# An encoder trunk on one core: two weight splits moved behind a product, and the last tiles' scaling handed from VectorE to ScalarE

## The chip, the cores and the metric

The kernel runs on one core of one Trainium2 chip. The metric is device time in microseconds (us) of one execution; the figure for a kernel is the median of its runs. The engines of the core are named as the profile names them: PE (TensorE, matmuls), PEld (its weight loads), DVE (VectorE), ACT (ScalarE), POOL (GpSimd) and SP (SyncE, which issues most DMAs).

## The reference

Two sequences of 512 tokens with 1024 features each go through two layers in float32. Layer 0 mixes tokens by a two-dimensional Fourier transform, layer 1 by attention; each is followed by an MLP with a squared ReLU. At the end comes a norm.

```python
def sq_relu_mlp(h, w_up, w_down):
    a = jnp.maximum(h @ w_up, 0)
    return (a * a) @ w_down

def trunk(x, ...):
    for i in range(DEPTH):          # DEPTH = 2
        j = i // N_MIXERS
        if i % N_MIXERS == 0:
            x = x + fourier_mix(rms_norm(x, fourier_norm[j]), fourier_w_out[j])
        else:
            x = x + gqa_attention(rms_norm(x, attn_norm[j]), attn_w_qkv[j], ...)
        x = x + sq_relu_mlp(rms_norm(x, mlp_norm[i]), mlp_w_up[i], mlp_w_down[i])
    return rms_norm(x, final_norm)

def rms_norm(x, g):
    y = x * lax.rsqrt(jnp.mean(x * x, axis=-1, keepdims=True) + EPS)
    return y * g
```

## The kernel before, in words

**Split operands.** A float32 product is made of three matmuls on halves: each operand is written as a high part (ACT copies it to `float32r`) and a low part (DVE subtracts the high part from the original). `split` (L82, L83) does both. Raw weights come into the pool `rawp` (tag `raw`, five buffers) by a DMA on SP's queue (`load_raw`, L91). A buffer of it is free again when its last reader has run, so a load stands in SP's queue, in order, until some DVE or ACT instruction has finished. The split weights go into the pool `wp` (`own()`) or into slots of the activations' pool (`lent()`); these show as `w` and `u` in the profile.

**The end of layer 0's MLP.** `second_product` multiplies the squared activations by `w_down` in a scheme of seven products over two-by-two blocks. Its work is a list of items, one for each output block `m` from 0 to 3 in each group of inner blocks. An item's `Sums.go` runs five products of 12 matmuls each, in the order `t1`, `t3`, `t2`, `b22`, `t4`. The first and the fourth share one accumulator in PSUM, the second and the fifth another: the fourth can start only when DVE has added the first's result into the residual (L1135), and the fifth only when it has added the second's. PE's order is fixed by hand there; that of the other engines is chosen by a scheduler, which takes the instructions as their inputs come ready and by the place at which the code states them. During an item the raw weights of the next are loaded, summed (L1202 to L1204, L1210) and split.

Attention's first weights (the third third of `w_qkv`, keys and values, four tiles of 128x1024) are wanted when this MLP ends. The last group's items 2 and 3 each call `late()`, which loads two of them and splits them at once:

```python
    def late():
        for _ in range(2):
            wkv.append(load_w(w_qkv[2, len(wkv)], home=lent))
```

Behind them in SP's queue come a table for the rotary embedding (`rope`) and the weights of the first queries (`w_qkv[0, ...]`, split into `own()` buffers). When a block `m` is finished, DVE adds (L1299, L1300) and `ready` makes attention's operands (`make_h`, L86 on ACT and L87 on DVE) and the squares for its norm (L154 on ACT, L156 on POOL).

**The tail.** The last 256 tokens of the second sequence are made with the tokens on the partitions: `x` holds tokens 256 to 383 ("third tile", accumulators `o[0]`, `o[1]`), `z` tokens 384 to 511 (three accumulators `oz`, whose matmuls at L1761 are PE's last). All orders are by hand there. On DVE: the two adds that complete `x` (L1771), four `ob.write` (L1706, each followed by a DMA on SP), `add_group(0)` and `add_group(1)` (L1766), the steps of a reciprocal square root (L131 on ACT, L132 to L136 on DVE), and `scaled` (L1682), which multiplies by the norm's factor and the norm's weights `gf` in one instruction. ACT makes the sums of squares (L1676) and scales half a row of `z` (L1795). Three of the four last output halves leave from SP's queue, one from ACT's.

Of the kernel before, what the change touches and what calls it, by code (L numbers as in the profile page):

```python
# [11 lines left out]
F32 = mybir.dt.float32  # L12
F32R = mybir.dt.float32r
BF16 = mybir.dt.bfloat16
AF = mybir.ActivationFunctionType
# [3 lines left out]
P = 128  # L19
D = 1024  # L20
# [16 lines left out]
SUM_GROUPS = ((0, 4), (4, 4), (8, 4), (12, 4)), ((0, 2), (2, 4), (6, 4), (10, 4))  # L37
# [3 lines left out]
def trunk_kernel(ctx, tc, x_in, xt_in, y_out, dcos, dsin, feat, rope, gfour, gcol, grow, gfin,  # L41
                 w_four, w_nyq, w_qkv, w_o, w_up, w_row2, w_row4, w_sum2, w_sum4, w_down):
    nc = tc.nc
# [17 lines left out]
    def slot(shape, dt):  # L61
        return act.tile(shape, dt, tag="u4", name=nm("u"))
# [4 lines left out]
    def small(n=4):  # L67
        return sm.tile([P, n], F32, tag="s", name=nm("s"), padded_shape=[P, 8])
# [12 lines left out]
    def split(dst_hi, dst_lo, src, eng=nc.vector):  # L81
        nc.scalar.copy(dst_hi, src)  # L82
        eng.tensor_sub(dst_lo, src, f32(dst_hi))  # L83
# [5 lines left out]
    def load_raw(src, shape=(P, 1024)):  # L89
        raw = rawp.tile(list(shape), F32, tag="raw", name=nm("raw"))  # L90
        nc.sync.dma_start(raw, src)  # L91
        return raw
# [14 lines left out]
    def lent():  # L107
        return slot([P, 1024], F32R), slot([P, 1024], F32R)

    def load_w(src, eng=nc.vector, parts=1, home=own):  # L110
        raw = load_raw(src)
        w = home()
        for i in range(parts):
            sl = slice(i * 1024 // parts, (i + 1) * 1024 // parts)
            split(w[0][:, sl], w[1][:, sl], raw[:, sl], eng)
        return w
# [9 lines left out]
    def rsqrt_steps(out, ss, n, inv, more=None):  # L126

        v, s, y = [small(n)[:, :n] for _ in range(3)]
        stt = nc.vector.scalar_tensor_tensor
        return [  # L130
            lambda: nc.scalar.activation(s, ss, AF.Sqrt, scale=inv, bias=eps if more is None else more),  # L131
            lambda: nc.vector.tensor_scalar(v, ss, inv, EPS if more is None else more, ALU.mult, ALU.add),  # L132
            lambda: nc.vector.reciprocal(v, v),
            lambda: nc.vector.tensor_mul(y, s, v),
            lambda: stt(s, y, -0.5, s, ALU.mult, ALU.mult),
            lambda: stt(out, s, 1.5, y, ALU.add, ALU.mult),  # L136
        ]
# [529 lines left out]
    with tc.manual_schedule(engines={ET.PE, ET.Activation, ET.DVE, ET.Pool, ET.SP}):  # L667
# [127 lines left out]
        blocks = Blocks(0)  # L795
# [26 lines left out]
        rows = []  # L822
# [290 lines left out]
        for r in last:  # L1113
            r.go()

    def second_product(l, blocks, rows, late=lambda: None, ready=lambda m: None):
        e, new = [], [True] * 4
        there = set()

# [200 lines left out]
        if there_later:  # L1320
            rows, sums = items[0]
# [18 lines left out]
        else:  # L1340
            rows, sums = items[0]
# [17 lines left out]

        for k, (rows, sums) in enumerate(items):  # L1360
            nrows, nsums = items[k + 1] if k + 1 < len(items) else ([], None)
            if sums.g == len(SUM_GROUPS[l]) - 1 and sums.m > 1:
                late()
            with tc.manual_schedule(engines={ET.PE}):
                for r in rows:
                    r.first()
                    if r.m == 3:
                        change("b11", 0, r.g)
                for r in nrows:
                    r.load()  # L1370
                if k:
                    sums.split_3()
                hook()
                for i, op in enumerate(("t1", "t3", "t2", "b22", "t4")):
                    sums.go(i)
                    if sums.m == 3:
                        change(op, 1, sums.g)
                    if i == 0 and nsums:
                        nsums.load()
                    if i == 1:  # L1380
                        for r in rows:
                            r.second()
                            if r.m == 3:
                                change("b21", 0, r.g)
                        hook()
                        for r in nrows:
                            r.split()
                    hook()
                    if there_later and k == 0 and i in (2, 4):
                        change(ROW[i // 4], 0, 0)  # L1390
                    if i == 2 and nsums:
                        nsums.sum_123()
                        nsums.split_12()
                    if i == 3 and nsums:
                        nsums.sum_4()
                        nsums.split_4()
            for r in rows:
                finish(r.m)
            finish(sums.m)


    hT, rs, wkv = [[], []], [], []
# [3 lines left out]
        rsqrt(r, sums(q), NT, 1.0 / D)  # L1406
        rs.append(r)

    def late():
        for _ in range(2):  # L1410
            wkv.append(load_w(w_qkv[2, len(wkv)], home=lent))

    def operands(q, m):
        for fo in range(2 * m, 2 * m + 2):
# [181 lines left out]
    late = [qr[1, 2 + i % 2][:, 2 + i // 2] for i in range(4)]  # L1596
# [8 lines left out]
    for n in range(1, len(heads) + 1):  # L1605
        pts, nxt = [], []
        for t in range(NT):
# [3 lines left out]
            if n in (3, 5, 7, 9) and t == 0:  # L1611
                i = (n - 3) // 2
# [107 lines left out]
    with tc.manual_schedule(engines={ET.PE, ET.Activation, ET.DVE, ET.Pool, ET.SP}):  # L1720
        oa, ob, oc, oe = OutT(0, 4), OutT(1, 2), Out(), Out(3)
        for fo in range(KC):
            project(0, fo, ws, [a[0] for a in ats])
            square(0, fo)
            oa.gain(fo)
        xtok = [tokens(2, KC), tokens(3, 6)]
        for fo in range(KC):
            project(1, fo, ws, [a[1] for a in ats], 256)
            square(1, fo, 256)
            ob.gain(fo)  # L1730
            if fo == 1:
                oa.root()
            if fo == 3:
                oa.spread()
            if fo > 3:
                oa.write(fo - 4)
        x = xtok[0]
        o = ps(), ps()
        cols = slice(2 * P, 3 * P)
        for k in range(len(ats)):  # L1740
            ak, wk = ats[k][1], ws[k]
            for i in range(2):
                sl = slice(i * 512, (i + 1) * 512)
                mm3(o[i], ak[0][:, cols], ak[1][:, cols], wk[0][:, sl], wk[1][:, sl], k == 0, k == len(ats) - 1)
            if k == 1:
                ob.root()
        ob.spread()
        z = xtok[1]
        groups = ((0, 512), (512, 768), (768, 1024))
        oz = [ps() for _ in groups]  # L1750
        mm = nc.tensor.matmul
        for i, (c0, c1) in enumerate(groups):
            out = oz[i][:, : c1 - c0]
            if i == 2:
                for k in range(2):
                    mm(oz[2][:, k * P : (k + 1) * P], xt(1, 6 + k)[:, 3 * P :], ident, start=k == 0, stop=False,
                       skip_group_check=True)
            for k in range(len(ats)):
                (ah, al), (wh, wl) = ats[k][1], ws[k]
                for n, (lh, rh) in enumerate(((ah, wh), (ah, wl), (al, wh))):  # L1760
                    mm(out, lh[:, 3 * P :], rh[:, c0:c1], start=k + n + i // 2 == 0,  # L1761
                       stop=k == len(ats) - 1 and n == 2, skip_group_check=i == 2)

        def add_group(i):
            sl = slice(*groups[i])
            nc.vector.tensor_add(z[:, sl], oz[i][:, : groups[i][1] - groups[i][0]], z[:, sl])  # L1766
            oe.square(z[:, sl], i)

        h0, h1 = slice(0, 512), slice(512, 1024)
        for i, sl in enumerate((h0, h1)):  # L1770
            nc.vector.tensor_add(x[:, sl], o[i], x[:, sl])  # L1771
        oc.square(x)
        root = oc.root()
        ob.write(0)
        ob.write(1)
        add_group(0)
        for step in root[:3]:
            step()
        ob.write(2)
        for step in root[3:]:  # L1780
            step()
        ob.write(3)
        add_group(1)
        y, part = [slot([P, D], F32) for _ in range(2)], small(1)[:, 0:1]
        oc.scaled(y[0], x[:, h0], h0)
        nc.sync.dma_start(y_out[2][:P, h0], y[0][:, h0])
        nc.vector.tensor_mul(y[1][:, h0], z[:, h0], gf[:, h0])
        nc.vector.tensor_add(part, oe.ss[:, 0:1], oe.ss[:, 1:2])
        nc.vector.tensor_scalar(part, part, 1.0 / D, EPS, ALU.mult, ALU.add)
        oe.square(oz[2][:, :256], 2)  # L1790
        oc.scaled(y[0], x[:, h1], h1)
        nc.sync.dma_start(y_out[2][:P, h1], y[0][:, h1])
        for step in rsqrt_steps(oe.r, oe.ss[:, 2:3], 1, 1.0 / D, part):
            step()
        nc.scalar.activation(y[1][:, h0], y[1][:, h0], AF.Copy, scale=oe.r)  # L1795
        nc.scalar.dma_start(y_out[2][P:, h0], y[1][:, h0])
        oe.scaled(y[1], z[:, 512:768], slice(512, 768))
        oe.scaled(y[1], oz[2][:, :256], slice(768, 1024))
        nc.sync.dma_start(y_out[2][P:, h1], y[1][:, h1])
# [130 lines left out]
```

## Time and profile before

| | us |
|---|---|
| median of three runs | 1701.62 |
| the three runs | 1701.62, 1701.74, 1700.10 |
| the profiled execution | 1699.59 |
| its span, from first to last instruction | 1697.8 |
| PE busy | 1681.2 (99%) |
| DVE busy | 1234.2 (73%) |
| ACT busy | 854.9 (50%) |
| POOL busy | 333.4 (20%) |

The span is what the trace covers; the remaining 1.8 us of the execution lie around it. Times "at 706" are us from the start of the span. In rows of a timeline the columns are the start, the duration, engine, line, operation, output and inputs, shapes, and in brackets the idle time just ahead with the instruction that ended it.

### The profile page before, as it was taken

Reading aid. Unit: us, or ns where it says so; the run is one execution under the profiler, and the core shown is the slowest. Engines: PE = TensorE matmul, PEld = TensorE weight load, DVE = VectorE, ACT = ScalarE, POOL = GpSimd, SP = SyncE. Lnnn points to the kernel's source line nnn. Section 1 sums busy time; section 2 is a strip of 40 time slices with the busy share of each in tenths; the row PEclk is TensorE's granted clock in tenths of the full one; section 3 lists DMA queues with packets and bytes.
Section 4 is the critical chain, followed back from the end, with each engine's and each line's share of the span. In section 5 each row is a group of like instructions: output and inputs, shape, how many; then the busy total and the mean of one; then the engine's idle time right before and its main releaser. Section 6 shows DMA issues by size and latency. Waiting matters only on the chain. (4 is left out here: it accounts for less than half of the span.)

```text
span 1697.8 us, 21868 instructions
## 1 busy us (share of the span) xinstructions
PE 1681.2 (99%) x7845; PEld 1395.0 (82%) x7845; DVE 1234.2 (73%) x1809; ACT 854.9 (50%) x1487; POOL 333.4 (20%) x304
## 2 busy tenths in 40 slices
PE   9999999999999999999999999999999999999998
PEld 7987888888788888788888888788888888888887
DVE  8788776557887879876588744687755479787864
ACT  7566444456242424457787714654444544344234
POOL 1321443221000000232344303014422200000002
PEclk9999999999999999999999999999999999999999
DMA  9643555449454644611000213335544686555322
GB/s 337 169 149 113 197 189 182 151 169 390 173 201 146 216 143 175 227 53 34 18 25 1 100 60 127 104 120 195 183 143 154 224 310 229 164 207 189 124 75 100
DMA packets 103679, 265.81 MB, mean 157 GB/s; under 512 B 10177, under 2 KB 10177, under 8 KB 103570
## 3 DMA queue, kind: packets, MB, share of 16 engines
q1 hardware_dynamic: 87410, 232.69, 39.4%
q10 hardware_dynamic: 14256, 25.96, 4.0%
q0 software_dynamic: 1904, 5.77, 1.7%
q8 instruction: 61, 1.00, 0.2%
q14 instruction: 48, 0.39, 0.1%
HBM read 189.40 MB, written 73.92 MB: 155 GB/s over the span
## 5 line engine op out<-in xcount | busy, mean ns | idle before, releaser
L869 PE MATMUL ps<-u,w 128*128 128x512 f32 x4656 | 1065.8, 389 | 4.9 <-DVE w L83 2.5
L869 PEld LDWEIGHTS ps<-u,w 128*128 128x128 f32 x4656 | 872.4, 188 | 189.7 <-DVE w L83 4.1
L82 ACT CAST w<-raw 128x1024 fp32r<-128x1024 f32 (+1 forms) x224 | 217.4, 981 | 444.1 <-PE ps L869 261.4
L83 DVE TENSOR_TENSOR w<-raw,w 128x1024 fp32r<-128x1024 f32 (+1 forms) x224 | 255.1, 1142 | 59.5 <-ACT w L82 59.0
L156 POOL TENSOR_TENSOR t<-t,t 128x512 f32<-128x512 f32 (+1 forms) x56 | 77.6, 1385 | 737.2 <-ACT t L154 681.3
L83 DVE TENSOR_TENSOR u<-u,u 128x1024 fp32r<-128x1024 f32 (+1 forms) x131 | 156.2, 1219 | 21.3 <-ACT u L82 20.6
L82 ACT CAST u<-u 128x1024 fp32r<-128x1024 f32 (+1 forms) x131 | 131.5, 1044 | 72.4 <-PE ps L869 48.8
L77 PE MATMUL ps<-u,u 128*128 128x512 f32 (+2 forms) x388 | 150.2, 387 | 0.4 <-DVE u L83 0.4
L1135 DVE TENSOR_TENSOR u<-ps,u 128x512 f32<-128x512 f32 x160 | 109.5, 686 | 54.0 <-PE ps L869 53.2
L79 PE MATMUL ps<-u,u 128*128 128x512 f32 (+2 forms) x388 | 144.4, 372 | 0.0
L78 PE MATMUL ps<-u,u 128*128 128x512 f32 (+2 forms) x388 | 144.2, 372 | 0.0
L869 PE MATMUL ps<-u,u 128*128 128x512 f32 x576 | 137.6, 390 | 0.6 <-DVE t L960 0.5
L869 PEld LDWEIGHTS ps<-u,u 128*128 128x128 f32 x576 | 107.9, 188 | 24.1 <-issue 0.9
L986 POOL TENSOR_TENSOR u<-u 128x512 f32<-128x512 f32 x28 | 36.6, 1309 | 401.4 <-ACT u L885 401.4
L83 DVE TENSOR_TENSOR u<-ps,u 128x512 fp32r<-128x512 f32 (+4 forms) x118 | 74.7, 649 | 19.6 <-ACT u L82 18.5
L79 PEld LDWEIGHTS ps<-u,u 128*128 128x128 f32 x388 | 73.1, 188 | 13.0
L77 PEld LDWEIGHTS ps<-u,u 128*128 128x128 f32 x388 | 73.3, 189 | 10.7 <-DVE u L83 0.6
L78 PEld LDWEIGHTS ps<-u,u 128*128 128x128 f32 x388 | 73.4, 189 | 10.5
L82 ACT CAST u<-ps 128x512 fp32r<-128x512 f32 (+4 forms) x118 | 65.6, 561 | 27.1 <-PE ps L79 11.6
L947 DVE TENSOR_TENSOR t<-ps,u 128x512 f32<-128x512 f32 x30 | 20.7, 690 | 79.8 <-PE ps L869 58.0
L852 DVE TENSOR_TENSOR u<-ps,u 128x512 f32<-128x512 f32 (+1 forms) x48 | 30.9, 645 | 64.4 <-PE ps L79 64.4
L77 PE MATMUL ps<-u,w 128*128 128x512 f32 (+2 forms) x192 | 65.1, 339 | 0.0
(244 smaller groups left out, 1987.0 us busy)
## 6 DMA issues: line engine op xcount, KB each, us to landing
raw<-w_up SPq DMA_DIRECT2D x82, 512.0 KB, 4.5
u<-spill_t SPq DMA_DIRECT2D x60, 512.0 KB, 5.9
raw<-w_sum SPq DMA_DIRECT2D x56, 512.0 KB, 4.3
u<-spill_b SPq DMA_DIRECT2D x45, 512.0 KB, 5.2
spill_t<-u SPq DMA_DIRECT2D x87, 256.0 KB, 2.0
spill_b<-t ACTq DMA_DIRECT2D x60, 256.0 KB, 3.0
raw<-w_row SPq DMA_DIRECT2D x28, 512.0 KB, 4.1
park<-u SPq DMA_DIRECT2D x24, 512.0 KB, 3.2
```

The source lines that it names most:

```text
L77: nc.tensor.matmul(out, lh, rh, start=first, stop=False)
L78: nc.tensor.matmul(out, lh, rl, start=False, stop=False)
L79: nc.tensor.matmul(out, ll, rh, start=False, stop=last)
L82: nc.scalar.copy(dst_hi, src)
L83: eng.tensor_sub(dst_lo, src, f32(dst_hi))
L156: nc.gpsimd.tensor_add(acc[q][:, :n], acc[q][:, :n], s[:, :n])
L852: nc.vector.tensor_add(x[:, :n], o[:, :n], x[:, :n])
L869: nc.tensor.matmul(o, w[x][:, sl], h[k][y], start=first and k + i == 0, stop=k == n - 1 and i == 2, skip_group_check=not first)
L947: nc.vector.tensor_add(u2, ob, t[:, 0])
L986: eng.tensor_sub(t[:, 0], b12, b11)
L1135: nc.vector.tensor_add(x, o, x)
```

## The change

The first part cuts `late` in two. `late(False)` at the start of items 2 and 3 only loads two raw tiles; `late(True)` splits them, and is stated behind the fourth product of the same item, after the next item's `sum_4` and `split_4`. The second part reorders the tail. The third tile is multiplied by `gf` in one 128x1024 instruction ahead of `add_group(0)`; its two halves are then scaled by the norm's factor on ACT, in place of the two `scaled` on DVE. The second half's DMA goes to ACT's queue, `add_group(1)` moves into the steps of the first root, and `ob.write(3)` moves behind the sums for the second root, whose steps are cut in two around ACT's scaling.

```diff
-    def second_product(l, blocks, rows, late=lambda: None, ready=lambda m: None):
+    def second_product(l, blocks, rows, late=lambda split_them: None, ready=lambda m: None):
...
-            if sums.g == len(SUM_GROUPS[l]) - 1 and sums.m > 1:
-                late()
+            ending = sums.g == len(SUM_GROUPS[l]) - 1 and sums.m > 1
+            if ending:
+                late(False)
...
                     if i == 3 and nsums:
                         nsums.sum_4()
                         nsums.split_4()
+                    if i == 3 and ending:
+                        late(True)
...
-    def late():
+    wraw = []
+
+    def late(split_them):
         for _ in range(2):
-            wkv.append(load_w(w_qkv[2, len(wkv)], home=lent))
+            if split_them:
+                wkv.append(lent())
+                split(*wkv[-1], wraw[len(wkv) - 1])
+            else:
+                wraw.append(load_raw(w_qkv[2, len(wraw)]))
...
         oc.square(x)
+        y, part = [slot([P, D], F32) for _ in range(2)], small(1)[:, 0:1]
         root = oc.root()
         ob.write(0)
         ob.write(1)
+        nc.vector.tensor_mul(y[0], x, gf)
         add_group(0)
         for step in root[:3]:
             step()
         ob.write(2)
+        add_group(1)
         for step in root[3:]:
             step()
-        ob.write(3)
-        add_group(1)
-        y, part = [slot([P, D], F32) for _ in range(2)], small(1)[:, 0:1]
-        oc.scaled(y[0], x[:, h0], h0)
+        nc.scalar.activation(y[0][:, h0], y[0][:, h0], AF.Copy, scale=oc.r)
         nc.sync.dma_start(y_out[2][:P, h0], y[0][:, h0])
         nc.vector.tensor_mul(y[1][:, h0], z[:, h0], gf[:, h0])
         nc.vector.tensor_add(part, oe.ss[:, 0:1], oe.ss[:, 1:2])
         nc.vector.tensor_scalar(part, part, 1.0 / D, EPS, ALU.mult, ALU.add)
         oe.square(oz[2][:, :256], 2)
-        oc.scaled(y[0], x[:, h1], h1)
-        nc.sync.dma_start(y_out[2][:P, h1], y[0][:, h1])
-        for step in rsqrt_steps(oe.r, oe.ss[:, 2:3], 1, 1.0 / D, part):
+        ob.write(3)
+        root = rsqrt_steps(oe.r, oe.ss[:, 2:3], 1, 1.0 / D, part)
+        for step in root[:3]:
+            step()
+        nc.scalar.activation(y[0][:, h1], y[0][:, h1], AF.Copy, scale=oc.r)
+        nc.scalar.dma_start(y_out[2][:P, h1], y[0][:, h1])
+        for step in root[3:]:
             step()
         nc.scalar.activation(y[1][:, h0], y[1][:, h0], AF.Copy, scale=oe.r)
         nc.scalar.dma_start(y_out[2][P:, h0], y[1][:, h0])
```

What the scheduler made of the first part is seen in DVE's order. This is DVE in item 2, before; `raw_5751` and `raw_5757` are the first two tiles of `w_qkv`, the `w_` rows split the next item's weights, and L1135 are the adds that free PE's accumulators:

```order
L1204 TENSOR_TENSOR raw_5784<-raw_5784,raw_5782 128x512
L83 TENSOR_TENSOR u_5754<-raw_5751,u_5753 128x1024
L1135 TENSOR_TENSOR u_4004<-ps_5786,u_4004 128x512
L83 TENSOR_TENSOR u_5760<-raw_5757,u_5759 128x1024
L83 TENSOR_TENSOR w_5818<-raw_5814,w_5818 128x1024
L1135 TENSOR_TENSOR t_3730<-ps_5800,t_3730 128x512
L1210 TENSOR_TENSOR raw_5782<-raw_5782,raw_5814 128x512
```

and the same place on DVE in the changed kernel, where the two tiles are `raw_5751` and `raw_5753`:

```order
L1204 TENSOR_TENSOR raw_5776<-raw_5776,raw_5774 128x512
L83 TENSOR_TENSOR w_5810<-raw_5806,w_5810 128x1024
L1135 TENSOR_TENSOR u_4004<-ps_5778,u_4004 128x512
L1210 TENSOR_TENSOR raw_5774<-raw_5774,raw_5806 128x512
L83 TENSOR_TENSOR u_5831<-raw_5751,u_5830 128x1024
L1135 TENSOR_TENSOR t_3730<-ps_5792,t_3730 128x512
L83 TENSOR_TENSOR w_5827<-raw_5774,w_5827 128x512
L83 TENSOR_TENSOR u_5835<-raw_5753,u_5834 128x1024
```

The next item's weights and L1210 now stand ahead of the two splits, which move down by three and by four rows. A little further, where item 2 ends and item 3 begins, DVE has before (`raw_6493` is the first weight of the queries, `raw_5861` and `raw_5867` the third and fourth tile; `ps_5878` and `ps_5892` are the results of item 3's first and second product):

```order
L1299 TENSOR_TENSOR u_3668<-u_3668,t_3730 128x512
L83 TENSOR_TENSOR w_6495<-raw_6493,w_6495 128x1024
L87 SCALAR_TENSOR_TENSOR u_5857<-u_3668,gc,u_5857 128x512
L83 TENSOR_TENSOR u_5864<-raw_5861,u_5863 128x1024
L1135 TENSOR_TENSOR u_4118<-ps_5878,u_4118 128x512
L83 TENSOR_TENSOR u_5870<-raw_5867,u_5869 128x1024
L1135 TENSOR_TENSOR u_4118<-ps_5892,u_4118 128x512
```

and now (`ps_5870` and `ps_5884` are those two results):

```order
L1299 TENSOR_TENSOR u_3668<-u_3668,t_3730 128x512
L1135 TENSOR_TENSOR u_4118<-ps_5870,u_4118 128x512
L87 SCALAR_TENSOR_TENSOR u_5857<-u_3668,gc,u_5857 128x512
L83 TENSOR_TENSOR w_6495<-raw_6493,w_6495 128x1024
L83 TENSOR_TENSOR u_5926<-raw_5861,u_5925 128x1024
L1135 TENSOR_TENSOR u_4118<-ps_5884,u_4118 128x512
L83 TENSOR_TENSOR u_5930<-raw_5863,u_5929 128x1024
```

The add of the first product moved ahead of the queries' weight and of a split; the add of the second stands behind both as before. PE's and POOL's orders are unchanged, and SP's is changed in the tail alone. ACT's casts follow DVE's new order. One thing of SP's queue is not seen in its order: the third tile's buffer is now the one that L1210 frees, the fourth's the one that the first of the deferred splits frees, and the load of `raw_6493` waits for the second deferred split, where before it waited for the split of `raw_5782`.

In the tail, ACT had before (L1676 are sums of squares, `s_14149` is the third tile's factor, `s_14151` the last tile's):

```order
L1676 ACTIVATE t_14604,s_14150<-u_14312 128x256
L1676 ACTIVATE t_14614,s_14150<-ps_14540 128x256
L131 ACTIVATE s_14619<-s_14150,s_14608 128x1
L1795 ACTIVATE u_14607<-u_14607,s_14151 128x512
L1796 DMA y<-u_14607 128x512
```

and has now (L1685 is that L1676, L1808 that L1795):

```order
L1685 ACTIVATE t_14603,s_14150<-u_14312 128x256
L1794 ACTIVATE u_14583<-u_14583,s_14149 128x512
L1685 ACTIVATE t_14613,s_14150<-ps_14540 128x256
L131 ACTIVATE s_14618<-s_14150,s_14585 128x1
L1804 ACTIVATE u_14583<-u_14583,s_14149 128x512
L1805 DMA y<-u_14583 128x512
L1808 ACTIVATE u_14584<-u_14584,s_14151 128x512
L1809 DMA y<-u_14584 128x512
```

Two scalings and one DMA issue came to ACT, one of the scalings ahead of the third sum of squares and one ahead of the last scaling.

## The prediction

> **What bounds the kernel.** I read the page's parts 1 and 4 first, then PE's waits, then PE's and DVE's rows around the two places that the change touches.
>
> ```profile
> span 1697.8 us, 21868 instructions
> PE 1681.2 (99%) x7845; PEld 1395.0 (82%) x7845; DVE 1234.2 (73%) x1809; ACT 854.9 (50%) x1487; POOL 333.4 (20%) x304
> ```
>
> PE is idle for 1697.8 - 1681.2 = 16.6 us in all, so a saving must come out of these or of the end behind PE's last matmul. From 700 us on PE waits for others only three times:
>
> ```profile
> PE ps L869 <- DVE u L1135: 1.5, 1, 1.5
> PE ps L869 <- DVE u L224: 0.9, 1, 0.9
> PE ps L1524 <- POOL t L1518: 0.2, 1, 0.2
> ```
>
> The columns are the total, the number of times and the longest. The first lies in item 3 of the MLP's last group:
>
> ```profile
> 647.80 58.87 PE L869 MATMUL ps<-u,w 128*128 128x512 f32 x259
> 708.14 5.74 PE L869 MATMUL ps<-u,w 128*128 128x512 f32 x24 [1.47 <-DVE u L1135]
> 713.72 0.39 PE L77 MATMUL ps<-u,u 128*128 128x512 f32 x1
> ```
>
> One matmul starts (58.87 - 0.39) / 258 = 0.2267 us behind the other, so the next would have started at 647.80 + 259 x 0.2267 = 706.51. It is the first of the fourth product, which waits until DVE has added the first product's result. Twenty-four matmuls on, attention would have begun at 711.95, not at 713.72: the stall costs 1.77 us. Its cause is in DVE's queue:
>
> ```profile
> 690.75 1.21 DVE L83 TENSOR_TENSOR u<-raw,u 128x1024 fp32r<-128x1024 f32 x1
> 691.89 0.68 DVE L1135 TENSOR_TENSOR u<-ps,u 128x512 f32<-128x512 f32 x1
> 692.49 1.94 DVE L83 TENSOR_TENSOR u<-raw,u 128x1024 fp32r<-128x1024 f32 x1
> ...
> 697.59 0.69 DVE L83 TENSOR_TENSOR w<-raw,w 128x512 fp32r<-128x512 f32 x1 [0.16 <-ACT w L82]
> ...
> 699.93 1.22 DVE L1300 TENSOR_TENSOR u<-u,t 128x1024 f32<-128x1024 f32 x1
> 701.06 0.68 DVE L1135 TENSOR_TENSOR u<-ps,u 128x512 f32<-128x512 f32 x1
> 701.78 0.69 DVE L1299 TENSOR_TENSOR u<-u,t 128x512 f32<-128x512 f32 x1
> 704.46 1.23 DVE L83 TENSOR_TENSOR w<-raw,w 128x1024 fp32r<-128x1024 f32 x1 [1.99 <-ACT w L82]
> 705.61 0.74 DVE L87 SCALAR_TENSOR_TENSOR u<-u,gc,u 128x512 fp32r<-128x512 f32 x1
> 706.27 1.22 DVE L83 TENSOR_TENSOR u<-raw,u 128x1024 fp32r<-128x1024 f32 x1
> 707.40 0.68 DVE L1135 TENSOR_TENSOR u<-ps,u 128x512 f32<-128x512 f32 x1
> ```
>
> The add that PE wants is the row at 707.40. Its product was done at 706.51 - 24 x 0.2267 = 701.07 and a little, but ahead of it stands the first weight of the queries, for whose high part DVE idles 1.99 us, because ACT waits for the load:
>
> ```profile
> 703.38 1.05 ACT L82 CAST w<-raw 128x1024 fp32r<-128x1024 f32 x1 [4.88 <-DMA raw<-w_qkv]
> 698.30 2.06 SPq L91 DMA_DIRECT2D raw<-w_qkv  x2
> ```
>
> The second row is the issue: 703.38 - 698.30 = 5.08 us from issue to cast.
>
> The tail, from PE's last matmuls to the last DMA:
>
> ```profile
> 1684.54 1.27 DVE L1706 TENSOR_TENSOR u<-u,ps 128x512 f32<-128x512 f32 x2
> 1686.88 0.69 DVE L1766 TENSOR_TENSOR u<-ps,u 128x512 f32<-128x512 f32 x1 [1.07 <-PE ps L1761]
> 1688.61 0.16 DVE L134 TENSOR_TENSOR s<-s,s 128x1 f32<-128x1 f32 x1 [0.19 <-ACT s L131]
> 1689.67 0.42 DVE L1766 TENSOR_TENSOR u<-ps,u 128x256 f32<-128x256 f32 x1
> 1690.01 0.74 DVE L1682 SCALAR_TENSOR_TENSOR u<-u,s,gf 128x512 f32<-128x512 f32 x1
> 1690.66 0.68 DVE L1787 TENSOR_TENSOR u<-u,gf 128x512 f32<-128x512 f32 x1
> 1691.52 0.74 DVE L1682 SCALAR_TENSOR_TENSOR u<-u,s,gf 128x512 f32<-128x512 f32 x1
> 1692.18 0.20 DVE L132 TENSOR_SCALAR s<-s,s 128x1 f32<-128x1 f32 x1
> 1693.67 0.48 DVE L1682 SCALAR_TENSOR_TENSOR u<-ps,s,gf 128x256 f32<-128x256 f32 x1
> 1690.60 0.36 ACT L1676 ACTIVATE t<-ps 128x256 bf16<-128x256 f32 x1
> 1693.27 0.72 ACT L1795 ACTIVATE u<-u,s 128x512 f32<-128x512 f32 x1 [1.27 <-DVE s L136]
> 1694.02 0.39 ACTq L1796 DMA_DIRECT2D y<-u  x1
> 1694.18 0.33 SPq L1799 DMA_DIRECT2D y<-u  x1
> ```
>
> From 1686.88 to 1694.15 (1693.67 + 0.48) DVE idles once, 0.19 us: these 7.27 us are DVE's own instructions, one behind the other, and the last DMA leaves 0.03 us later. ACT has holes all along.
>
> **Part one, the splits.** Nothing is added or removed; two pairs of casts and subtractions move. The early loads are issued as before. DVE's new order from 690.75 on is: weight split, add, L1210, deferred split, add, half-size split, deferred split. With starts spaced as in the rows (1.14 for 1024 columns, 0.60 for 512) that is 3 x 1.14 + 4 x 0.60 = 5.82, to 696.57. Until here it is the old work without the 0.73 by which the split at 692.49 exceeded the one at 690.75. Next come L87 and an add (0.66 and 0.60), a weight split (1.14), L1300 (1.13), the add that waits (0.72 from 701.06 to 701.78) and L1299 (0.60): 4.85, to 701.42. There now stands the first product's add, whose result is there, and it ends at 702.1, 4.4 us before PE wants it at 706.51. The deferred splits cost nothing: their reader is attention's first product at 711.95, some 15 us later.
>
> What is late next is the second product's add. The fifth product wants it at 706.51 + 12 x 0.2267 = 709.23, and it still stands behind the queries' weight. That load now waits for the second deferred split, so it is issued at about 696.6, not 698.30. I keep 5.08 us to the cast: 701.7. Behind the cast (0.96 to the next row's start, as from 703.38 to 704.34) ACT scales an operand (0.72), which DVE's L87 needs: 703.4. L87, the weight split, a split and the add take 0.66 + 1.14 + 1.14 + 0.68: DVE is done at 707.0, 2.2 us early. The third tile's load, now behind L1210, goes out at about 693.2 in place of 692.0, and its reader in this chain comes at 705.2, 12 us on.
>
> So the whole 1.77 us should go. From below the bound is the new wait at the fifth product, which eats it from a landing at 703.9 on; from above, the 1.77 itself. I take 1.77. It reaches the end because PE waits for only 0.9 + 0.2 us more behind this place; the nearest margin that could eat it is the softmax loop's, where POOL's 0.2 us wait shows how close it runs, and its inputs come from PE, which shifts them too.
>
> These four loads come closer together (693.2 to 696.6 in place of 692.0 to 698.3). One more price is open, DVE against POOL:
>
> ```profile
> 689.04 1.79 DVE L1204 TENSOR_TENSOR raw<-raw,raw 128x512 f32<-128x512 f32 x1
> 692.05 1.29 POOL L156 TENSOR_TENSOR t<-t,t 128x512 f32<-128x512 f32 x1 [1.77 <-ACT t L154]
> 706.67 4.18 POOL L156 TENSOR_TENSOR t<-t,t 128x512 f32<-128x512 f32 x2 [13.32 <-ACT t L154]
> ```
>
> An instruction of 512 columns took 1.79 us in place of 0.68, and the split at 692.49 took 1.94 in place of 1.21, both beside a POOL addition. By these rows a collision costs DVE 0.73 to 1.11, and the two additions of the last row, which will come some 1.7 us earlier and so beside the weight split and the add, at most 2.2: the margin, just. The Trainium skill's page "SBUF — State Buffer", section "Who interferes with whom", says that a VectorE instruction with two SBUF inputs and a GpSimd one that reads SBUF exclude each other for a whole instruction. The trace agrees in kind. By that rule two collisions could cost 2 x 1.29 = 2.6, and PE would wait 0.4 us at the fifth product: a sum of 2.9 in place of 3.3.
>
> **Part two, the tail.** The product with `gf` costs one 128x1024 instruction (1.22 by the L1300 row, 1.14 to the next start). It starts at 1685.74, when the two L1706 are through, in DVE's wait of 1.07 us for PE, and lets the next start at 1686.88: exactly PE's release. Cost 0 to 0.1. Out of DVE's 7.27 us fall two L1682 (1690.01 to 1690.66 and 1691.52 to 1692.18: 0.65 + 0.66). The 0.19 wait for ACT's root goes as well, since the 256-column add (0.34) now stands ahead of it. The other rows only change places. Sum 1.50.
>
> ACT gets two scalings (0.72 each by L1795) and one more DMA issue (0.39). The first waits for the factor, which comes at about 1689.3 (three root steps behind the moved add), and ends by 1690.0; the third sum of squares follows and ends by 1690.4. DVE wants that at 1692.18 - 1.50 = 1690.68: 0.3 us to spare. The second scaling and its issue end at about 1691.7, when the last factor arrives. So ACT's last scaling ends at 1692.5, and its DMA leaves beside SP's at 1692.7; the transfers behind are the same, 1.5 us earlier. If ACT ran 0.72 later, the DVE end would lose 0.4, so the bounds are 1.0 and 1.6. I take 1.50.
>
> **The sum.** 1.77 + 1.50 = 3.27 us. The profiled execution took 1699.59 and would take 1696.3; the median of the runs stands 2.03 above it, so 1701.62 - 3.27 = 1698.35, or 1698.3. The measurement tells about 0.2% from no change, which is 3.4 us: the forecast lies right at that edge.
>
> **The rivals.**
> 1. The wait moves to the fifth product. For it: DVE still idles for the same load there, and POOL's additions fall in. Against it: 2.2 us of margin. With half the gain left, 0.9 + 1.5 = 2.4: 1699.2.
> 2. The 1.77 is lost further on, in the softmax loop or at L224. For it: POOL's wait at L1524. Against it: one wait of 0.2 us in a loop that PE feeds. Then only the tail counts: 1700.1.
> 3. ACT becomes the tail's bound through the added scaling and issue. Against it: the holes above. 1.77 + 1.0 = 2.8: 1698.8.
> 4. Slower: the queries' weight lands late, because four 512 KB loads now follow in 3.4 us. A landing beyond 703.9 (7.3 us after issue) costs PE one for one. The kernel gets slower than before only from 707.2 on, and by over 0.2% from 710.6, 14 us after issue. L91's loads took 11.7 us at most:
>
> ```profile
> DMA to landing us min/median/max: 2.5/4.3/11.7
> ```
>
> **How the numbers follow.** The main case has 0.65, rival 1 0.14, rival 2 0.09, rival 3 0.08, rival 4 0.04. In the main case 3.27 lies just below the edge of 3.4, and the three runs spread over 1.6 us, so I give 0.40 of its 0.65 to faster. A little of rival 3 goes there too: faster 0.42, same 0.54, slower 0.04. The main case alone is 1697.0 to 1699.2; for eight in ten I take in rivals 1 and 2 and the spread of runs: 1696.7 to 1700.4.
>
> **What would show it.** Right: PE's only long waits behind 700 us are those for L224 and L1524; L77 begins near 711.95; DVE's wait for the queries' weight stands behind the first add; the last SP issue comes 5.8 us behind the last L1761, where it was 7.3. Wrong: a wait for L1135 in the middle of item 3, an ACT row that ends DVE's idle time ahead of the second L132, or a new PE wait in attention.

## The result, and the profile after

| | us |
|---|---|
| before, median of 17 runs | 1700.06 (1699.27 to 1701.74) |
| after, median of 17 runs | 1697.31 (1696.56 to 1698.75) |
| ratio after to before | 0.9984, 95% interval 0.9978 to 0.9990 |
| the profiled execution of after, and its span | 1697.05, 1695.3 |

The change takes 2.75 us away; the interval makes that 1.7 to 3.7 us. The first three runs of before, with their median of 1701.62, had come out high: over 17 runs it stands at 1700.06.

The page of after, parts 0 and 1, and what PE waits for behind 700 us:

```profile
span 1695.3 us, 21868 instructions
PE 1681.1 (99%) x7845; PEld 1395.1 (82%) x7845; DVE 1231.3 (73%) x1808; ACT 854.8 (50%) x1489; POOL 334.6 (20%) x304
```

```profile
PE ps L869 <- DVE u L224: 0.9, 1, 0.9
PE ps L1533 <- POOL t L1527: 0.2, 1, 0.2
```

PE has the same work. The wait for L1135 is gone; the two others are those of before (line numbers behind `late` are 9 to 13 higher now). The end of the MLP in PE's timeline:

```profile
699.12 13.12 PE L869 MATMUL ps<-u,w 128*128 128x512 f32 x57
712.08 0.39 PE L77 MATMUL ps<-u,u 128*128 128x512 f32 x1
```

Fifty-seven matmuls at 0.2267 us end at 699.12 + 12.92 = 712.04; attention begins 0.04 later, 1.64 us ahead of the first trace. DVE there, then the load that it waits for, on SP and ACT:

```profile
692.54 1.18 DVE L1210 TENSOR_TENSOR raw<-raw,raw 128x512 f32<-128x512 f32 x1
...
695.98 1.22 DVE L83 TENSOR_TENSOR u<-raw,u 128x1024 fp32r<-128x1024 f32 x1
...
701.98 0.69 DVE L1135 TENSOR_TENSOR u<-ps,u 128x512 f32<-128x512 f32 x1
704.44 0.75 DVE L87 SCALAR_TENSOR_TENSOR u<-u,gc,u 128x512 fp32r<-128x512 f32 x1 [1.78 <-ACT u L86]
705.11 1.22 DVE L83 TENSOR_TENSOR w<-raw,w 128x1024 fp32r<-128x1024 f32 x1
706.25 2.32 DVE L83 TENSOR_TENSOR u<-raw,u 128x1024 fp32r<-128x1024 f32 x1
708.49 0.68 DVE L1135 TENSOR_TENSOR u<-ps,u 128x512 f32<-128x512 f32 x1
```

```profile
697.23 2.72 SPq L91 DMA_DIRECT2D raw<-w_qkv  x2
702.74 1.05 ACT L82 CAST w<-raw 128x1024 fp32r<-128x1024 f32 x1 [5.71 <-DMA raw<-w_qkv]
```

The first product's add (701.98) now stands ahead of the wait for the queries' weight and ends at 702.67; the fourth product is due at 699.12 + 33 x 0.2267 = 706.60, 3.9 us later. The second's (708.49) ends at 709.17. PE's fifth product is due at 699.12 + 45 x 0.2267 = 709.32, so 0.15 us of margin is left.

The tail, DVE, then ACT, SP and PE:

```profile
1684.51 1.22 DVE L1786 TENSOR_TENSOR u<-u,gf 128x1024 f32<-128x1024 f32 x1
1685.66 0.69 DVE L1775 TENSOR_TENSOR u<-ps,u 128x512 f32<-128x512 f32 x1
...
1688.77 0.68 DVE L1715 TENSOR_TENSOR u<-u,ps 128x512 f32<-128x512 f32 x1
1689.54 0.21 DVE L132 TENSOR_SCALAR s<-s,s 128x1 f32<-128x1 f32 x1
...
1691.04 0.48 DVE L1691 SCALAR_TENSOR_TENSOR u<-ps,s,gf 128x256 f32<-128x256 f32 x1
```

```profile
1689.03 0.38 ACT L1685 ACTIVATE t<-ps 128x256 bf16<-128x256 f32 x1 [0.28 <-PE ps L1770]
...
1691.64 0.35 ACTq L1809 DMA_DIRECT2D y<-u  x1
```

```profile
1691.55 0.33 SPq L1812 DMA_DIRECT2D y<-u  x1
```

```profile
1687.26 1.67 PE L1770 MATMUL ps<-w,u 128*128 128x256 f32 x12
```

From the first add to SP's last issue it takes 1691.55 - 1685.66 = 5.89 us, where it was 7.30: 1.41 less. ACT's last issue comes 0.09 us later and is now the end, so 1.32 us is gained. ACT's third sum of squares starts when PE's last matmul ends (1687.26 + 1.67 = 1688.93), and DVE waits 0.09 us for it ahead of the last root.

### The profile page after: what moved, and what is told of

It is laid out like the page before. It is cut to its first block, busy times and chain, and to the rows that moved or that the text cites. A ratio compares the mean times of both kernels' runs of the same rounds, so it can differ in the third digit from the quotient of the medians.

```text
span 1695.3 us, 21868 instructions
## 1 busy us (share of the span) xinstructions
PE 1681.1 (99%) x7845; PEld 1395.1 (82%) x7845; DVE 1231.3 (73%) x1808; ACT 854.8 (50%) x1489; POOL 334.6 (20%) x304
## 5 line engine op out<-in xcount | busy, mean ns | idle before, releaser
L156 POOL TENSOR_TENSOR t<-t,t 128x512 f32<-128x512 f32 (+1 forms) x56 | 77.8, 1389 | 738.9 <-ACT t L154 683.0
L1135 DVE TENSOR_TENSOR u<-ps,u 128x512 f32<-128x512 f32 x160 | 109.5, 686 | 53.5 <-PE ps L869 53.0
```

The lines of the kernel that those rows point to most:

```text
L156: nc.gpsimd.tensor_add(acc[q][:, :n], acc[q][:, :n], s[:, :n])
L1135: nc.vector.tensor_add(x, o, x)
```

## The experiments

**Each part by itself.** In `splits_only` the tail is the text of before; in `tail_only` the splits are.

> Part one alone: the two split pairs moved, the tail as before. Theory A (the stall's 1.7 us reaches the end, save what a later place eats): PE shows no wait for L1135 in item 3, attention begins 1.7 us earlier, and the kernel is 1.2 to 1.7 us faster than before. Rival B (the stall's time is lost before the tail): the first matmul of the tail is less than 0.5 us earlier and the time is within 0.5 us of before. Separately: in the trace with both parts PE lost 0.4 us again between 1389 and 1418 us (layer 1's MLP, where DVE waits for w_sum loads). If that comes from the new order, this trace loses 0.4 us there too; if it comes from how the loads happen to land, it need not.

> Part two alone: the splits as before. Theory A: the last DMA issue comes 2.6 us behind PE's last matmul, where it was 4.0 us; the kernel is 1.4 us faster (1.3 to 1.5), since nothing else moves. Rival C (ACT's added scaling and issue bound the end): 1.0 us or less, and DVE waits for ACT ahead of the last root. The stall of 1.77 us at the fourth product of item 3 is still there. Between 1389 and 1418 us nothing is lost if the loss of 0.4 us belongs to the new order of the splits.

| | median, us | before beside it | ratio, 95% interval |
|---|---|---|---|
| splits_only | 1698.86 (11 runs) | 1699.82 (33 runs) | 0.9991, 0.9982 to 1.0000 |
| tail_only | 1698.46 (11 runs) | 1699.82 (33 runs) | 0.9991, 0.9982 to 1.0000 |

0.96 and 1.36 us: together 2.3, near the 2.75 of both. Each interval reaches from 0 to 3.1 us, so these times alone tell neither part from no change, nor one part from the other; what each is worth rests on the traces. The tail gives what was expected. The last issue in `tail_only` is ACT's:

```profile
1692.94 0.36 ACTq L1800 DMA_DIRECT2D y<-u  x1
```

It comes 2.99 us behind the start of PE's last matmul (1689.95), where in the first trace it was 1694.18 - 1689.88 = 4.30, so 1.31 less. The splits give less than expected. PE's timelines, `tail_only` (old order of the splits) first, then `splits_only`:

```profile
699.33 7.41 PE L869 MATMUL ps<-u,w 128*128 128x512 f32 x32
707.55 5.74 PE L869 MATMUL ps<-u,w 128*128 128x512 f32 x24 [0.81 <-DVE u L1135]
713.13 0.39 PE L77 MATMUL ps<-u,u 128*128 128x512 f32 x1
```

```profile
699.28 13.05 PE L869 MATMUL ps<-u,w 128*128 128x512 f32 x56
712.16 0.39 PE L77 MATMUL ps<-u,u 128*128 128x512 f32 x1
```

With the old order attention was due at 699.33 + 56 x 0.2267 = 712.03 and began 1.10 us late, not 1.77. With the new one it was due at 711.98 and began 0.18 late. So the stall itself differs between executions; the next two runs put that to the test.

**Before and after once more.** Both kernels unchanged, for a second trace of each.

> The kernel before, a second look. In the trace of tail_only, whose splits are as before, the stall at the fourth product of item 3 was 1.0 us instead of 1.77, since the queries' weight was cast earlier, and 0.6 us were lost between 1389 and 1418 us. Theory K (both come from how the loads land, and the first trace of before was one draw): this trace shows a stall other than 1.77 us, between 0.8 and 1.8, and a loss of 0.3 to 0.7 us between 1389 and 1418 us, of which the first trace had none. Rival L (they belong to the kernel): 1.77 us again, and no loss there.

> The kernel after, a second look. Theory K: no stall at the fourth product, since its add stands some 4 us early; at the fifth product between 0 and 0.3 us of wait, since its add is done 0.1 us early or late; a loss of 0.3 to 0.7 us between 1389 and 1418 us again. Rival L: exactly the rows of the first trace.

Before again, then after again:

```profile
699.25 7.42 PE L869 MATMUL ps<-u,w 128*128 128x512 f32 x32
708.04 5.76 PE L869 MATMUL ps<-u,w 128*128 128x512 f32 x24 [1.38 <-DVE u L1135]
713.64 0.39 PE L77 MATMUL ps<-u,u 128*128 128x512 f32 x1
```

```profile
699.21 13.28 PE L869 MATMUL ps<-u,w 128*128 128x512 f32 x57
712.32 0.39 PE L77 MATMUL ps<-u,u 128*128 128x512 f32 x1
```

That is 1.69 us late (due at 711.95) and 0.19 (due at 712.13). The old order has cost 1.77, 1.69 and 1.10 us in three traces, 1.5 in the mean, and the cast of the queries' weight explains the difference: 703.38, 703.28 and 702.79. The new order has cost 0.04, 0.18, 0.19 and, in `tail_less` below, 0.32, with that cast at 702.74, 702.80, 702.98 and 703.15; 0.2 in the mean. (The two traces of `sums_first` below, with the same code in layer 0, add 0.35 and 0.12, and the mean stays.) The difference is 1.3 us.

The second thing that differs lies far behind the change, in layer 1's MLP. DVE's first L1202 near 1386 us waits for a load of `w_sum`; here in the first trace of before, in `before_again` and in after:

```profile
1386.81 0.43 DVE L1202 TENSOR_TENSOR raw<-raw,raw 128x256 f32<-128x256 f32 x1 [1.53 <-DMA raw<-w_sum]
```

```profile
1387.97 0.43 DVE L1202 TENSOR_TENSOR raw<-raw,raw 128x256 f32<-128x256 f32 x1 [2.77 <-DMA raw<-w_sum]
```

```profile
1385.49 0.43 DVE L1202 TENSOR_TENSOR raw<-raw,raw 128x256 f32<-128x256 f32 x1 [1.92 <-DMA raw<-w_sum]
```

The table sets this wait beside PE's loss, the time from the 6440th to the 6600th matmul of the program minus the same in the first trace of before:

| | splits | DVE's wait, us | PE's loss, us |
|---|---|---|---|
| before | old | 1.53 | 0 |
| before_again | old | 2.77 | 1.15 |
| tail_only | old | 2.18 | 0.69 |
| after | new | 1.92 | 0.44 |
| splits_only | new | 2.27 | 0.95 |
| after_again | new | 2.06 | 0.87 |
| tail_less | new | 1.75 | 0.11 |
| defer2, defer3 (below) | mixed | 2.22, 2.51 | 0.63, 1.29 |
| no_pool_defer2 (below) | mixed | 1.55 | 0.23 |

Roughly, what the wait has beyond 1.5 us PE loses, with either order. So the 0.44 us that after seems to lose against the first trace is no cost of the change: that first trace had the shortest wait of all. Theory K holds in kind: both losses differ between executions of one order. Its 0.3 to 0.7 us between 1389 and 1418 us were too narrow (1.15 and 0.87 came), and the 1.69 us of stall by itself would hardly tell it from rival L; it is `tail_only`'s 1.10 that does.

**One pair of the two.** `defer2` keeps only item 2's deferral, `defer3` only item 3's. The edit is against the kernel after; the comments give the numbers for `defer3`:

```diff
             if ending:
                 late(False)
+                if sums.m == 3:      # defer3: == 2
+                    late(True)
...
-                    if i == 3 and ending:
+                    if i == 3 and ending and sums.m == 2:      # defer3: == 3
                         late(True)
```

> Both parts, but only item 2's pair is deferred; item 3's two splits are stated at once. On DVE that puts both of item 3's splits ahead of the second product's add, where one stands now. Theory D (the prediction's margin of 2.2 us at the fifth product): the add still comes in time, no wait, 2.7 us faster than before as with both pairs deferred. Theory E (the trace after: add done at 709.17, wanted at about 709.3, a margin of 0.1 to 0.2 us): the extra split takes 1.1 to 1.7 us, PE waits 1.0 to 1.6 us for L1135 at the fifth product, and the kernel is only 1.1 to 1.7 us faster than before.

> Both parts, but only item 3's pair is deferred; item 2's two splits are stated at once. DVE's order keeps the queries' weight ahead of the first product's add, and only one 1024-column split less stands between them. Theory A (the stall is the sum of what stands ahead of the first add): of 1.77 us about 1.77 - 1.14 = 0.6 us stays as a wait for L1135 at the fourth product, and the kernel is about 2.75 - 0.6 = 2.1 us faster than before. Rival F (item 3's pair alone makes the stall): no wait, 2.7 us faster. Rival G (item 2's pair alone makes it): the whole 1.77 us stays, 1.0 to 1.4 us faster.

`defer2` has a median of 1699.99 us against 1699.82 before (1.0001, 0.9992 to 1.0009): no gain is seen, with an interval from 1.4 us faster to 1.5 slower. PE and DVE there:

```profile
699.22 10.36 PE L869 MATMUL ps<-u,w 128*128 128x512 f32 x45
711.38 3.01 PE L869 MATMUL ps<-u,w 128*128 128x512 f32 x12 [1.79 <-DVE u L1135]
714.23 0.39 PE L77 MATMUL ps<-u,u 128*128 128x512 f32 x1
```

```profile
706.16 4.56 DVE L83 TENSOR_TENSOR u<-raw,u 128x1024 fp32r<-128x1024 f32 x2
710.64 0.68 DVE L1135 TENSOR_TENSOR u<-ps,u 128x512 f32<-128x512 f32 x1
```

The fourth product starts on time, and the fifth waits: attention, due at 712.14, begins 2.09 us late. One more split ahead of the second add has moved the stall on by one product and made it longer. The prediction's margin of 2.2 us (theory D) is refuted; theory E gave the place, and its 1.0 to 1.6 us were too little, since the two splits took 4.56 us and not the 3.4 to 4.0 that it counted with (2.32 and 1.1 to 1.7 more). By the stalls, 1.5 before and 2.09 here, and with the tail's 1.3, some 0.7 us should still be gained; that lies inside the interval.

`defer3` has 1697.62 us against 1699.82 (0.9986, 0.9977 to 0.9995): 2.2 us faster, with 2.1 expected; the interval of 0.9 to 3.9 us would also allow the other two theories, so the trace decides. The fourth product still waits, though in the trace for 0.28 us and not 0.6:

```profile
699.32 13.14 PE L869 MATMUL ps<-u,w 128*128 128x512 f32 x56
712.30 0.39 PE L77 MATMUL ps<-u,u 128*128 128x512 f32 x1
```

The weight's cast came at 703.07, 0.31 us ahead of the first trace of before, and with that the sum holds (1.77 - 1.14 - 0.31 = 0.32). So theory A's sum of what stands ahead of the add fits. Item 3's pair alone brings most of what the splits give, since 0.28 us of stall lie within the 0.04 to 0.35 of both pairs; item 2's alone only hands the stall to the fifth product. What item 2's pair adds to item 3's, these runs don't show.

**Why the splits are long.** `no_pool_defer2` is `defer2` without four of POOL's additions of squares (`add=False` leaves the addition out):

```diff
-            square(q, fo)
+            square(q, fo, add=q == 1 or fo not in (3, 4, 5, 6))
```

> defer2 without four of POOL's additions of squares in this stretch (the norm's sum lacks four of eight terms). Theory P (the long DVE rows come from POOL's additions): L1204 takes 0.69 instead of 1.78 us, the two splits ahead of the second add 2.35 instead of 4.56 us together, the add is done by 709.1 us or earlier, PE's wait at the fifth product falls from 1.8 us to 0 to 0.1, and the kernel is 2.3 to 3.0 us faster than before, where defer2 gained nothing. Rival Q (they are long for another reason, such as the loads that land there): the rows, the wait of 1.8 us and the time of defer2 stay.

It has 1697.30 us against 1700.49 before (0.9984, 0.9975 to 0.9993): 3.2 us faster, where 2.3 to 3.0 were expected (the interval is 1.2 to 4.3). With DVE's order of `defer2`:

```profile
689.43 0.68 DVE L1204 TENSOR_TENSOR raw<-raw,raw 128x512 f32<-128x512 f32 x1
...
704.57 2.35 DVE L83 TENSOR_TENSOR u<-raw,u 128x1024 fp32r<-128x1024 f32 x2
706.84 0.68 DVE L1135 TENSOR_TENSOR u<-ps,u 128x512 f32<-128x512 f32 x1
```

```profile
699.23 13.31 PE L869 MATMUL ps<-u,w 128*128 128x512 f32 x58
712.38 0.39 PE L77 MATMUL ps<-u,u 128*128 128x512 f32 x1
```

The rows are as short as theory P said, the second add is done at 707.52, and PE does not wait. The add starts 3.8 us earlier than in `defer2`: 2.2 because the two splits are shorter, 1.6 because the queries' weight is cast earlier (701.06 and not 702.65); its load leaves 1.4 earlier, since L1204 and L1210 ahead of it are no longer stretched. The additions cost `defer2` all that the splits could have given.

**What bounds the tail now.** `tail_less` is the kernel after without one product on DVE; ACT reads `z` instead:

```diff
-        nc.vector.tensor_mul(y[1][:, h0], z[:, h0], gf[:, h0])
...
-        nc.scalar.activation(y[1][:, h0], y[1][:, h0], AF.Copy, scale=oe.r)
+        nc.scalar.activation(y[1][:, h0], z[:, h0], AF.Copy, scale=oe.r)
```

> The kernel after without one DVE instruction of the tail, the product of the first half of z with gf (0.61 us; that output lacks gf). Theory H (behind the change the end hangs on PE's last matmul, ACT's third sum of squares and the root): the last issue still comes 2.6 us behind PE's last matmul, DVE waits 0.6 to 0.7 us for ACT ahead of the last root, and at most 0.1 us is gained on the kernel after. Rival M (the end still hangs on DVE's queue): 0.6 us earlier, 2.0 us behind PE's last matmul.

Its median is 1697.86 us against 1700.49 (0.9987, 0.9978 to 0.9995), so no more is gained than with the kernel after. In its tail PE's last matmul ends at 1688.95 and ACT's third sum of squares begins at 1689.05. DVE's last root, then SP's last issue:

```profile
1689.56 0.21 DVE L132 TENSOR_SCALAR s<-s,s 128x1 f32<-128x1 f32 x1 [0.43 <-ACT t L1685]
```

```profile
1691.57 0.33 SPq L1811 DMA_DIRECT2D y<-u  x1
```

DVE stands idle for 0.43 us there (and 0.18 us a little earlier, so that the 0.61 of the product are all idle now), the last root starts where it did, and SP's last issue still comes 2.6 us behind PE. Theory H holds: in the tail the change has used up what DVE's queue could give, and the end now hangs on PE, the third sum of squares, and the root.

**An attempt on the other wait.** `sums_first` is the kernel after with the raw weights of the sums issued ahead of the residuals in layer 1:

```diff
         def load(self):
+            if l:
+                self.x, self.y = sums_raw(self.m, self.g, self.n)
             for q in range(NSEQ):
                 residual(q, self.m)
-            self.x, self.y = sums_raw(self.m, self.g, self.n)
+            if not l:
+                self.x, self.y = sums_raw(self.m, self.g, self.n)
```

> The kernel after, and in layer 1's MLP the raw weights of an item's sums are issued ahead of its residuals (one MB of park in two loads) instead of behind the first of them. Theory N (the loss of 0 to 1.2 us at 1389 to 1418 us comes from the second w_sum load, which shares the DMA engines with the two park loads ahead of it): DVE's L1202 waits 1 us or more less there than in the traces so far (1.5 to 2.8 us), PE loses less than 0.1 us between 1389 and 1418 us, and the median is 0.3 to 0.8 us below the kernel after's, which so few runs cannot tell for certain. Rival O (the load is late for its buffer, or the residuals are then late): the wait stays within 0.3 us, or PE waits elsewhere by as much.

> A second look at sums_first, since the loss between 1389 and 1418 us differs from one execution to the next: under theory N less than 0.1 us again, under rival O something between 0 and 1.2 us.

It has 1697.48 us against 1699.69 (0.9984, 0.9975 to 0.9993), no better than the kernel after. The wait at the first sums went, but in one of the two traces the next sums (L1205 here) had it:

```profile
1389.07 0.42 DVE L1205 TENSOR_TENSOR raw<-raw,raw 128x256 f32<-128x256 f32 x1 [1.41 <-DMA raw<-w_sum]
```

PE lost 1.54 us there in that execution and gained 0.17 in the other. Theory N, which wanted less than 0.1 us in both, failed in one of the two. That row suggests that the order of the loads only chooses which of them is late; one trace does not show it, and how to cure the wait stays open.

## Why the prediction was right, and where it was not

1. **The time.** 1698.3 was forecast and 1697.31 came. Two errors stand against each other in it: the base of 1701.62 was 1.56 us above the median of 17 runs, and the sum of 3.27 was 0.52 above the measured 2.75. That they partly cancel is luck.
2. **The stall goes entirely.** At its place, yes. Its size was the mis-sized term: 1.77 us came from one trace, and three give 1.5 in the mean, because it grows with the landing of the queries' weight.
3. **The first add at 702.1.** It came at 702.67 (701.98 + 0.69), still 3.9 us early. L1210 took 1.18 us beside a POOL addition, 0.5 more than counted.
4. **The second add at 707.0, 2.2 us early.** This step failed: 709.17, with 0.15 to spare. The load left at 697.23 and not 696.6, since it waits for the second deferred split, which L1210 had made late (0.6); from issue to cast it took 5.51 us and not 5.08 (0.4); and the split at 706.25 took 2.32 in place of 1.21 (1.1). Together 2.1. The prediction had priced the POOL collision and called the margin "just", but carried the landing over unchanged from the old order. Why the load took longer stays open: in the six traces with both pairs moved it took 5.5 to 5.8 us, but in `defer2` and `no_pool_defer2`, where the loads follow as closely, 5.15 and 4.97. That the trace of after shows no wait at the fifth product is luck of the landing, with so little margin.
5. **Rival 1, a wait at the fifth product.** It occurs in small, 0.2 us in the mean. With 1.5 - 0.2 = 1.3 and the tail's 1.3 the sum is 2.6, beside the measured 2.75. The prediction's sentence on the Trainium skill's page "SBUF — State Buffer" ("Who interferes with whom") gave 0.4 us of wait and a sum of 2.9, nearer than the main sum. `no_pool_defer2` bears the rule out in kind; in size the collisions cost the DVE instruction 0.5 to 1.1 us each, less than the 1.29 us of a POOL addition (the last section shows why).
6. **Rival 2, the gain is lost further on.** The trace of after looks like it (0.4 us between 1389 and 1418), but the kernels with the old order lose as much there.
7. **The tail, 1.50.** 1.41 by SP's issue and 1.32 by ACT's, which is now last by 0.09. The product in DVE's wait cost nothing: the add follows it at 1685.66, as PE releases it. The 7.3 and 5.8 us that the prediction names as a sign count from this first add of the accumulators, and not from the last L1761: from the start of PE's last matmul SP's last issue comes 4.30 us behind before, 2.90 now.
8. **Rival 3, ACT bounds the tail.** Not ACT's added work: the third sum of squares starts 0.1 us behind PE's last matmul. What the prediction left out is that PE's end releases that sum of squares.
9. **Rival 4.** The landing came at 702.7 to 703.2 in the four traces of the new order above and at 703.2 and 703.8 in the two of `sums_first` (whose products came 0.4 and 0.8 us later than in after, too), short of the 703.9 from which it would have cost one for one; the collision brought the edge nearer, so that up to 0.35 us were paid already.

## What to carry to other kernels

When an instruction that waits for a load stands in an in-order queue ahead of one that the busiest engine wants, look where the wait lands after the move and count what still stands ahead of the next wanted instruction: here one split more (`defer2`) made a stall of 2.1 us one product later, longer than the one that was cured. Try the parts of a move one by one: here one of the two pairs brought most of the gain. A stall that ends with a DMA's landing has a spread, so its size should come from several executions; here 1.1 to 1.77 us. An old trace can also be lucky elsewhere, and a difference of 0.4 us far behind the change needs a second trace of the kernel before.

## What the runs showed of the hardware

The same load took 4.5 us from issue to cast in one execution (698.27 to 702.79, `tail_only`) and 5.1 in another (698.30 to 703.38, before) with nothing changed ahead of it, and 5.0 to 5.8 in the eight traces in which item 2's pair is deferred.

DVE's instruction with two inputs from SBUF was stretched beside a POOL addition (1.21 to 2.32 us), while the adds with one input in PSUM were not: L1135 took 0.68 at 708.49, between POOL's start at 706.02 and its end at 709.72:

```profile
706.02 3.70 POOL L156 TENSOR_TENSOR t<-t,t 128x512 f32<-128x512 f32 x2 [12.85 <-ACT t L154]
```

The price of such a meeting can be read from the ends. These are one addition in before and one in after:

```profile
688.68 1.60 POOL L156 TENSOR_TENSOR t<-t,t 128x512 f32<-128x512 f32 x1 [15.91 <-ACT t L154]
```

```profile
691.17 2.01 POOL L156 TENSOR_TENSOR t<-t,t 128x512 f32<-128x512 f32 x1 [0.83 <-ACT t L154]
```

L1204 in before ends at 689.04 + 1.79 = 690.83, 0.55 us behind the first; L1210 in after at 692.54 + 1.18 = 693.72, 0.54 behind the second. So in these rows DVE lost what was left of POOL's addition: 1.1 us where a DVE instruction with two SBUF inputs ran just ahead (L87 ahead of L1204), 0.5 where an L1135 did (ahead of L1210).
